# A two-layer hybrid attention block: score products in three float32r passes in place of plain float32

## The chip, the core and the metric

The kernel runs on one core of one Trainium2 chip. The core has five engines with queues of their own: TensorE (PE in the profile; its weight loads are listed apart as PEld), VectorE (DVE), ScalarE (ACT), GpSimd (POOL) and SyncE (SP), which here issues the transfers. Each engine takes its instructions in a fixed order and waits on semaphores for the others. Matrix products read SBUF, the 128-partition working memory, and write PSUM, eight banks of 512 float32 columns. The metric is the device time of one launch in microseconds, the median of several runs; lower is better.

## The reference, cut to what matters

Two layers over 512 tokens of width 1024, in float32. Each layer has an attention block with 16 heads of 64 (four with a top-k selection, four "stick-breaking", eight with a sliding window) and a gated feed-forward block. The score products are those between queries and keys, in four places:

```python
def _dsa(q, k, v, qi, ki, wi):                       # heads A, and the index heads
    ...
        rel = jax.nn.relu(jnp.einsum('bqhd,bsd->bqhs', qin, ki).astype(jnp.float32))
        score = jnp.einsum('bqh,bqhs->bqs', win.astype(jnp.float32), rel) * idx_scale
        ...
        _, sel = lax.top_k(score, n_sel)
        ...
        s = jnp.einsum('bqhd,bqkd->bhqk', qn, ks).astype(jnp.float32) * scale
...
def _stick_breaking(q, k, v):                        # heads B
    ...
        z = jnp.einsum('bqhd,bshd->bhqs', qn, k).astype(jnp.float32) * scale
...
def _swa_sinks(q, k, v, sinks):                      # heads C
    ...
        s = jnp.einsum('bqkgd,bskd->bkgqs', qn, kn).astype(jnp.float32) * scale
...
def reference(...):
    for l in range(DEPTH):
        ...
        x = x + g1 * _mixing(h, w_in[l], ..., w_o[l], cos, sin)
        h = _rms(x, ln2[l]) * (1 + sc2) + sh2
        x = x + g2 * _swiglu(h, w_gate[l], w_up[l], w_down[l])
    return x
```

## The kernel before, in words

Activations lie transposed, model dimension on the partitions and the 512 tokens along the free dimension. Every weight product is split: `load_w` (L535) fetches a chunk of weights into a `raw` slot, ScalarE copies it to float32r (the high part, L553) and VectorE subtracts (the low part, L554). `mm3` (L579) then does a product in three float32r passes: high by high, high by low, low by high. The activations are split the same way into `acth` and `actl`.

The score products are not split. After their projection, queries and keys are normalised and rotated on VectorE (`rope_apply`, L649), transposed by TensorE into a bank `w` (L255), and copied by ScalarE into float32 slots (L747, L748 for the index heads, L1016 and L1038 for heads C, L1142 and L1143 for heads A; `qk_run`, L871, scales those of heads B straight out of the product). A score product is then one float32 matmul with 64 rows (the head's dimension) and 128 to 512 columns of keys, or for heads B of queries, in `score` (L767), `headB` (L908), `unitC` (L1073) and `unitA` (L1167). Its bank `z` goes to ScalarE or VectorE: a relu and the weighted sum for the top-k search (L792, L793, sixteen rounds of eight on VectorE), the exponentials of heads B, the masked row maximum of heads C and A. The probabilities are transposed again (banks `t`) and multiplied by the values (bank `o`).

What sets the order: the class `Weaver` (L61) keeps a clock of its own, `now`, that each TensorE instruction moves by a price (L249), and a list of tasks. A task says how many nanoseconds its next step needs from now (the tables `LAT`, L52) and which banks; once its time has come, it goes ahead of the weight products, which fill the time between in packets of one `mm3`. So TensorE's order is fixed when the program is built. VectorE's own background work (the top-k rounds) is put in while its estimated backlog is under `SLACK`. SyncE issues transfers in order and waits for a free slot of the kind asked for; `wk` and `hid` share one pool of `WK` slots of 512 columns (L42, L208), used for modulation weights at the start (`mod_load`, L343), for queries, keys and selections in the attention, and for the hidden activations in the feed-forward block.

In the timeline, names give the tile: `z<-wk,wk` writes a score bank from two slots of that pool.

## Time and profile before

| | |
|---|---|
| median of 3 runs | 1319.72 us (1319.38 to 1322.63) |
| profiled execution: span from its first to its last instruction | 1314.4 us |
| TensorE busy | 1290.3 us, 98% |
| its weight loads | 1042.9 us, 79% |
| VectorE busy | 814.2 us, 62% |
| ScalarE busy | 540.0 us, 41% |
| chain that ended last | TensorE 95%, VectorE 2%, ScalarE 1% |
| read from memory | 149.34 MB |

The profile is one execution. For that execution the trace gives its span and no other time; the runs' median lies 5.3 us above the span, and that is the launch's time around the first and the last instruction. Matmuls are pipelined, so the busy time of TensorE counts overlaps and its own rate is read from the distance between starts. The stretches up to about 300 us and from 680 to 940 us are the two attention blocks; the rest is feed-forward.

### The profile page before, as it was taken

How to read it: one execution, taken by the hardware profiler on the slowest of the kernel's cores; microseconds unless marked ns; L12 is line 12 of the kernel's file. 1: busy time of each engine (PE TensorE's matmuls, PEld its weight loads, DVE VectorE, ACT ScalarE, POOL GpSimd, SP SyncE). 2: the span in 40 equal slices, each digit the busy share in tenths (PEclk: the TensorE clock that was granted, in tenths of full speed). 3: DMA queues.
4: the chain of work that ended last, by engine and by line, in shares of the span. 5: the costliest groups of instructions: out<-in, count | busy, mean ns of one | idle time of the engine just before them, and what ended most of it. 6: DMA issues, size and time to landing. Idle time of an engine off the chain costs nothing.

```text
span 1314.4 us, 19908 instructions
## 1 busy us (share of the span) xinstructions
PE 1290.3 (98%) x7572; PEld 1042.9 (79%) x7572; DVE 814.2 (62%) x2017; ACT 540.0 (41%) x1178; POOL 38.0 (3%) x51
## 2 busy tenths in 40 slices
PE   5999999999999999999999999999999999999998
PEld 3776787689888888888887868876998888888887
DVE  4898687857557667554259998786665533433423
ACT  4435576746322222222245466765452222222220
POOL 0000000002000000000020010000200000000000
PEclk9999999999999999999999999999999999999999
DMA  9852022220466667443222211121135422322311
GB/s 352 293 182 75 17 97 97 91 79 33 145 199 226 199 204 248 156 152 93 77 81 84 78 33 33 33 82 56 39 124 155 146 91 80 124 68 97 112 49 64
DMA packets 60000, 152.74 MB, mean 116 GB/s; under 512 B 7296, under 2 KB 7808, under 8 KB 59904
## 3 DMA queue, kind: packets, MB, share of 16 engines
q1 hardware_dynamic: 59904, 151.47, 35.2%
q8 instruction: 59, 0.97, 0.3%
q14 instruction: 37, 0.30, 0.1%
HBM read 149.34 MB, written 2.10 MB: 115 GB/s over the span
## 4 chain that ended last, share of the span: by engine, by line
PE 95%; DVE 2%; ACT 1%; issue 1%; DMA 0%; POOL 0%; POOLq 0%; SPq 0%; DVEq 0%; ACTq 0%
PE z L252 44%; PE mm L252 40%; PE o L252 4%; PE t L255 3%; PE w L255 2%; PE t L252 2%; PE w L252 1%; DVE sp L262 1%; DVE actl L262 1%; DVE e L262 0%; ACT ws L562 0%; DVE xT L262 0%; DMA xT<-in_x_dram 0%; ACT on L451 0%; ACT ws L553 0%
## 5 line engine op out<-in xcount | busy, mean ns | idle before, releaser
L252 PE MATMUL z<-acth,ws 128*128 128x512 f32 x1280 | 397.7, 390 | 0.0
L554 DVE TENSOR_TENSOR ws<-raw,ws 128x1024 fp32r<-128x1024 f32 (+3 forms) x190 | 208.0, 1098 | 249.1 <-ACT ws L553 249.0
L553 ACT CAST ws<-raw 128x1024 fp32r<-128x1024 f32 (+3 forms) x190 | 179.2, 948 | 334.7 <-PE z L252 157.2
L252 PEld LDWEIGHTS z<-acth,ws 128*128 128x128 f32 x1280 | 240.3, 188 | 49.8
L252 PE MATMUL mm<-hid,ws 128*128 128x512 f32 (+1 forms) x1212 | 271.8, 381 | 0.0
L252 PEld LDWEIGHTS mm<-hid,ws 128*128 128x128 f32 x1212 | 217.4, 188 | 48.5 <-issue 5.0
L252 PE MATMUL z<-actl,ws 128*128 128x512 f32 x640 | 249.0, 389 | 0.0
L252 PE MATMUL mm<-ws,acth 128*128 128x256 f32 (+2 forms) x704 | 151.8, 309 | 1.1 <-ACT acth L521 1.1
L252 PEld LDWEIGHTS z<-actl,ws 128*128 128x128 f32 x640 | 120.2, 188 | 24.5
L252 PE MATMUL mm<-acth,ws 128*128 128x256 f32 (+1 forms) x576 | 137.7, 325 | 0.5 <-DVE xT L262 0.5
L262 DVE SCALAR_TENSOR_TENSOR xT<-mm,mod,xT 128x512 f32<-128x512 f32 (+1 forms) x124 | 80.2, 660 | 68.5 <-PE mm L252 68.0
L252 PEld LDWEIGHTS mm<-ws,acth 128*128 128x128 f32 x704 | 111.0, 190 | 11.7 <-issue 5.6
L252 PEld LDWEIGHTS mm<-acth,ws 128*128 128x128 f32 x576 | 96.6, 190 | 14.3 <-issue 5.4
L252 PE MATMUL mm<-ws,actl 128*128 128x256 f32 (+2 forms) x352 | 104.0, 296 | 0.9 <-DVE actl L262 0.9
L252 PE MATMUL mm<-actl,ws 128*128 128x256 f32 (+1 forms) x288 | 91.8, 319 | 0.0
L291 ACT ACTIVATE e<-z 128x512 f32<-128x512 f32 x40 | 23.9, 599 | 159.6 <-PE z L252 159.6
L400 DVE SCALAR_TENSOR_TENSOR at<-nat,cs,at 128x512 f32<-128x512 f32 x98 | 73.1, 746 | 15.1 <-DMA nat<-in_w_mod_dram 14.8
L252 PEld LDWEIGHTS mm<-ws,actl 128*128 128x128 f32 x352 | 66.7, 190 | 1.6 <-DVE actl L262 1.5
L252 PE MATMUL z<-wk,wk 64*128 64x256 f32 (+3 forms) x192 | 57.4, 413 | 0.0
L252 PEld LDWEIGHTS mm<-actl,ws 128*128 128x128 f32 x288 | 54.9, 191 | 2.9
L793 DVE MATCH_REPLACE8 wk<-top,wk 128x256 f32<-128x256 f32 (+2 forms) x96 | 51.7, 543 | 0.0
L792 DVE MAX8 top<-wk 128x8 f32<-128x256 f32 (+2 forms) x96 | 50.8, 551 | 0.3
(213 smaller groups left out, 1411.0 us busy)
## 6 DMA issues: line engine op xcount, KB each, us to landing
raw<-in_w_gu_dram SPq DMA_DIRECT2D x88, 512.0 KB, 4.1
nat<-in_w_mod_dram SPq DMA_DIRECT2D x112, 256.0 KB, 3.4
raw<-in_w_dn_dram SPq DMA_DIRECT2D x48, 384.0 KB, 3.2
wk<-in_w_mod_dram SPq DMA_DIRECT2D x64, 256.0 KB, 5.5
raw<-in_w_nat_dram SPq DMA_DIRECT2D x16, 512.0 KB, 4.5
raw<-in_w_o_dram SPq DMA_DIRECT2D x16, 512.0 KB, 3.6
raw<-in_w_qk_dram SPq DMA_DIRECT2D x8, 512.0 KB, 4.4
raw<-in_w_mod_dram SPq DMA_DIRECT2D x8, 512.0 KB, 5.3
```

The costliest lines, as they stand in the source:

```text
L252: return self._done(T0.matmul(o, lhsT, rhs, **k), ns)
L255: return self._done(T0.transpose(o, i, idn), 109)
L262: ins = f(o, *a, **k)
L291: ins = S.activation(*a, **k)
L400: ins = V0.scalar_tensor_tensor(a, w, cs[:, k:k + 1], a, op0=OP.mult, op1=OP.add)
L553: ops = [S.copy(sp[:, 0, :n], raw[:, :n])]
L554: ops.append(V0.tensor_sub(sp[:, 1, :n], raw[:, :n], sp[:, 0, :n].bitcast(F32)))
L792: pinned(V0.max(top8, sc[:, :n]), n)
L793: pinned(V0.match_replace(sc[:, :n], top8, sc[:, :n], TAKEN), n)
```

## The change

Queries and keys are held in two float32r slots each, a high and a low part, and every score product is an `mm3`. A new helper does the split: ScalarE copies (or scales) out of PSUM into the high part, VectorE subtracts it from the source into the low part. The slots come from the `hid` kind, so more of the shared pool are in use, and `WK` grows from 17 to 25; the space comes out of a scratch area of the DMA set to 256 bytes. The values of heads B move from half of a `ws` slot to two `wk` slots. Comments are dropped. The prices in the `Weaver` and its `LAT` stay as they are, but the order follows from them anew, since a product now counts three instructions.

```diff
-NWS, NRAW, WK = 6, 5, 17
+NWS, NRAW, WK = 6, 5, 25
...
+    def split_to(hl, src, scale=None):
+
+        h, lo = hl
+        if scale is None:
+            S.copy(h, src)
+            V.tensor_sub(lo, src, h.bitcast(F32))
+        else:
+            S.mul(h, src, scale)
+            V.scalar_tensor_tensor(lo, src, scale, h.bitcast(F32), op0=OP.mult, op1=OP.subtract)
...
-                S.copy(a["kiT"][:, t * P:(t + 1) * P], tb[:, 2 * P:3 * P])
-                S.copy(a["qiT"][t].rearrange("p a b -> p (a b)"), tb[:, :2 * P])
+                split_to([k[:, t * P:(t + 1) * P] for k in a["kiT"]], tb[:, 2 * P:3 * P])
+                split_to([q[:, t * 256:(t + 1) * 256] for q in a["qiT"]], tb[:, :2 * P])
...
-                T.matmul(sb[:, :n], a["qiT"][t][hp, h // 2], a["kiT"][hp, :n], start=True, stop=True)
+                q0 = t * 256 + h // 2 * P
+                mm3(sb[:, :n], *(q[hp, q0:q0 + P] for q in a["qiT"]), *(k[hp, :n] for k in a["kiT"]), True, True)
...
-                a[name] = [slot("wk") for _ in range(2)]
-                yield from tr_run(ws, a["hs"], range(KO), lambda m, pb: S.mul(a[name][m], pb, scale), "qk")
+                a[name] = [[slot("hid") for _ in range(2)] for _ in range(2)]
+                yield from tr_run(ws, a["hs"], range(KO), lambda m, pb: split_to(a[name][m], pb, scale), "qk")
...
+        def vb_pre():
+            v = [slot("wk") for _ in range(2)]
+            a["vb"] = [v[t // 2][:, t % 2 * 256:(t % 2 + 1) * 256] for t in range(NT)]
...
-                        T.matmul(zb[:, a0:a0 + w], kT[:, j * P:(j + 1) * P], qT[:, j * P:], start=(a0 == 0), stop=False,
-                                 skip_group_check=True)
+                        mm3(zb[:, a0:a0 + w], *(v[:, j * P:(j + 1) * P] for v in kT), *(v[:, j * P:] for v in qT), a0 == 0,
+                            False, skip_group_check=True)
...
-                    S.copy(a["kcT"][g][:, t * P:(t + 1) * P], tb[:, g * P:(g + 1) * P])
+                    split_to([k[:, t * P:(t + 1) * P] for k in a["kcT"][g]], tb[:, g * P:(g + 1) * P])
...
-                    S.copy(a["qcT"][t][:, 2 * hf:2 * hf + 2].rearrange("p a b -> p (a b)"), tb[:, :256])
+                    split_to([q[:, 256 * hf:256 * hf + 256] for q in a["qcT"][t]], tb[:, :256])
...
-                    T.matmul(sb[:, hh * 256:hh * 256 + n], a["qcT"][t][hp, hs_[hh] // 2], a["kcT"][g][hp, k0:k0 + n],
-                             start=True, stop=True)
+                    q0 = hs_[hh] // 2 * P
+                    mm3(sb[:, hh * 256:hh * 256 + n], *(q[hp, q0:q0 + P] for q in a["qcT"][t]),
+                        *(k[hp, k0:k0 + n] for k in a["kcT"][g]), True, True)
...
-                S.copy(a["kaT"][:, t * P:(t + 1) * P], tb[:, 2 * P:3 * P])
-                S.copy(a["qaT"][t].rearrange("p a b -> p (a b)"), tb[:, :2 * P])
+                split_to([k[:, t * P:(t + 1) * P] for k in a["kaT"]], tb[:, 2 * P:3 * P])
+                split_to([q[:, t * 256:(t + 1) * 256] for q in a["qaT"]], tb[:, :2 * P])
...
-                T.matmul(sb[:, :n], a["qaT"][t][hp, h // 2], a["kaT"][hp, :n], start=True, stop=True)
+                q0 = t * 256 + h // 2 * P
+                mm3(sb[:, :n], *(q[hp, q0:q0 + P] for q in a["qaT"]), *(k[hp, :n] for k in a["kaT"]), True, True)
...
-    nc = _bacc.Bacc("TRN2", target_bir_lowering=False, num_devices=1)
+    nc = _bacc.Bacc("TRN2", target_bir_lowering=False, num_devices=1, dynamic_dma_scratch_size=256)
```

Three places in the order. The first is TensorE's at a unit of heads C in layer 0 (second half of the heads, third token block): the transposes of a query block into a bank `w`, and the next unit's two products into a bank `z`. Before:

```order
L255 MATMUL w_2399<-cst,nat_2274 128x128 x2
L252 MATMUL o_2403<-vc_1104,pT_2382 64x64 x4
L255 MATMUL t_2408<-cst,p_2295 128x128 x2
L252 MATMUL z_2443<-wk_1109,wk_1582 128x256 x2
L252 MATMUL o_2403<-vc_1104,pT_2411 64x64 x4
```

And of the changed kernel, the same place, which is also where a product comes soonest behind the split that it reads (`hid_1654` is the low part that VectorE makes from `w_2547`):

```order
L255 MATMUL w_2547<-cst,nat_2404 128x128 x2
L255 MATMUL t_2552<-cst,p_2430 128x128 x2
L252 MATMUL z_2587<-hid_1159,hid_1653 128x256
L252 MATMUL z_2587<-hid_1160,hid_1653 128x256
L252 MATMUL z_2587<-hid_1159,hid_1654 128x256
L252 MATMUL z_2587<-hid_1159,hid_1653 128x256
L252 MATMUL z_2587<-hid_1160,hid_1653 128x256
L252 MATMUL z_2587<-hid_1159,hid_1654 128x256
```

Two products of 64 rows have become six passes, and between the transposes into `w` and the first pass stand two other transposes alone, where four short products with the values stood as well.

The second is VectorE's at that place in the changed kernel; `p_2530` are the two masked row maxima (ISA) of the unit before, `nat_2561` the next query block.

```order
L262 ISA p_2530,cmx_2464<-z_2529,cst,rc_1648 128x256
L262 ISA cmx_2464 128x1
L262 ISA p_2530,cmx_2464<-z_2529,cst,rc_1648 128x256
L262 ISA cmx_2464 128x1
L262 TENSOR_TENSOR ocv_2496<-ocv_2496,ocd_2498 128x4
L262 TENSOR_REDUCE cvv_2559<-rt_2557 128x4
L262 TENSOR_TENSOR nat_2561<-mm_2420,gn 128x256
L262 SCALAR_TENSOR_TENSOR cnb_2465<-cmx_2464,nsk 128x2
L262 TENSOR_TENSOR hid_1654<-w_2547,hid_1653 128x256
```

The subtraction into `hid_1654` is new here and stands behind the row maxima and two instructions of the next query block.

The third is SyncE's at the start, from the second chunk of the first weight product on (`wk` are modulation weights, 256 KB each; `raw` weight chunks; `rp` the rope table; `gn` gains; `nsk` sinks). Before:

```order
L543 DMA raw_150<-in_w_nat_dram 128x972
L349 DMA wk_152<-in_w_mod_dram 128x512
L543 DMA raw_169<-in_w_nat_dram 128x648
L837 DMA rp<-in_rope_dram 128x512
L718 DMA gn<-in_gains_dram 128x512
L719 DMA nsk<-in_sinks_dram 128x16
L349 DMA wk_154<-in_w_mod_dram 128x512
L349 DMA wk_156<-in_w_mod_dram 128x512
```

Of the changed kernel:

```order
L543 DMA raw_150<-in_w_nat_dram 128x972
L349 DMA wk_152<-in_w_mod_dram 128x512
L349 DMA wk_154<-in_w_mod_dram 128x512
L349 DMA wk_156<-in_w_mod_dram 128x512
L349 DMA wk_158<-in_w_mod_dram 128x512
L349 DMA wk_160<-in_w_mod_dram 128x512
L349 DMA wk_162<-in_w_mod_dram 128x512
L349 DMA wk_164<-in_w_mod_dram 128x512
L349 DMA wk_166<-in_w_mod_dram 128x512
L543 DMA raw_169<-in_w_nat_dram 128x648
L349 DMA wk_171<-in_w_mod_dram 128x512
```

and further on, behind the fourth and the fifth group:

```order
L543 DMA raw_549<-in_w_nat_dram 128x1024
L543 DMA raw_554<-in_w_nat_dram 128x1024
L847 DMA rp<-in_rope_dram 128x512
L728 DMA gn<-in_gains_dram 128x512
L729 DMA nsk<-in_sinks_dram 128x16
```

The third group of modulation weights (from `wk_152` on) is no longer broken off behind its first transfer, the rope table and what follows it moved behind the fourth and fifth group and four chunks more.

## Rows read from the trace of the kernel before

**Rows 1.** The page: its span, and the chain that ended last, by engine.
```profile
span 1314.4 us, 19908 instructions
...
PE 95%; DVE 2%; ACT 1%; issue 1%; DMA 0%; POOL 0%; POOLq 0%; SPq 0%; DVEq 0%; ACTq 0%
```

**Rows 2.** Windows: stretch, its length, busy us per engine (instructions), clock, DMA share, GB/s.
```profile
40.00:140.00 100.00, 97.43 (x621) 69.35 (x620) 91.72 (x258) 49.32 (x108) 4.67 (x7) 0.98 0.43 152
680.00:800.00 120.00, 117.45 (x785) 91.25 (x785) 111.19 (x312) 66.03 (x154) 5.58 (x9) 1.00 0.17 54
```

**Rows 3.** Tile z: count, ns min/median/max, first and last start us, forms.
```profile
L252 PE MATMUL z<-wk,wk x192: 272/376/693, 96.6 to 857.4; 64*128 64x256 f32 x112, 64*128 64x128 f32 x48, 64*128 64x384 f32 x16, 64*128 64x512 f32 x16
L252 PE MATMUL z<-wk,ws x112: 272/482/693, 53.7 to 909.1; 64*128 64x256 f32 x32, 64*128 64x384 f32 x32, 64*128 64x512 f32 x32, 64*128 64x128 f32 x16
```

**Rows 4.** Timeline of PE: start us, us, line, out<-in, rows*columns, moving operand, count.
```profile
302.03 0.58 PE L252 MATMUL z<-ones,on 128*128 128x1 f32 x4
302.48 0.36 PE L252 MATMUL mm<-acth,ws 128*128 128x256 f32 x1
...
302.79 0.40 PE L252 MATMUL mm<-acth,ws 128*128 128x256 f32 x2
...
303.15 0.40 PE L252 MATMUL mm<-acth,ws 128*128 128x256 f32 x2
...
346.96 0.62 PE L252 MATMUL z<-acth,ws 128*128 128x512 f32 x2
...
347.64 0.62 PE L252 MATMUL z<-acth,ws 128*128 128x512 f32 x2
```

**Rows 5.** Timeline of PE: score products and what follows each.
```profile
181.62 1.13 PE L252 MATMUL z<-wk,wk 64*128 64x256 f32 x4
182.68 0.51 PE L252 MATMUL o<-vc,pT 128*64 128x64 f32 x10
...
188.90 0.71 PE L252 MATMUL z<-wk,wk 64*128 64x128 f32 x4
189.54 0.68 PE L252 MATMUL o<-vc,pT 128*64 128x64 f32 x15
...
257.44 1.12 PE L252 MATMUL z<-wk,ws 64*128 64x512 f32 x2
258.50 0.73 PE L252 MATMUL mm<-hid,ws 128*128 128x512 f32 x2
```

**Rows 6.** Groups of DVE by form: count, busy us, mean ns, idle before them.
```profile
L262 DVE TENSOR_TENSOR actl<-w,acth 128x512 fp32r<-128x512 f32 x8 | 5.5, 686 | 2.1 <-ACT acth L985 2.0
...
L262 DVE TENSOR_TENSOR actl<-w,acth 128x256 fp32r<-128x256 f32 x8 | 3.3, 418 | 0.9 <-ACT acth L985 0.9
```

**Rows 7.** Timeline, all engines: transposes of an output, the copy, the subtraction.
```profile
907.79 0.44 PE L255 MATMUL w<-cst,on 128*128 128x128 f32 x2
...
908.26 0.37 ACT L985 CAST acth<-w 128x256 fp32r<-128x256 f32 x1 [0.63 <-PE w L255]
...
908.67 0.42 DVE L262 TENSOR_TENSOR actl<-w,acth 128x256 fp32r<-128x256 f32 x1 [0.64 <-ACT acth L985]
```

**Rows 8.** Timeline of SP: issue of transfers.
```profile
18.94 0.33 SPq L349 DMA_DIRECT2D wk<-in_w_mod_dram  x1
...
22.39 9.77 SPq L349 DMA_DIRECT2D wk<-in_w_mod_dram  x15
```

**Rows 9.** Windows: the stretch in which the first weights arrive.
```profile
20.00:40.00 20.00, 19.97 (x115) 11.60 (x116) 14.06 (x37) 8.41 (x17) 0.00 (x0) 1.00 1.05 395
```

**Rows 10.** Chain of waits in order of time: start us, us, what.
```profile
45.21 0.94 DVE rt L262 x3
...
47.68 1.13 DVE ws L554
...
48.98 0.33 PE w L255
```

**Rows 11.** The page, DMA issues: count, KB each, us to landing.
```profile
wk<-in_w_mod_dram SPq DMA_DIRECT2D x64, 256.0 KB, 5.5
```

More of the change, by code (lines that the diff above doesn't have):

```diff
@@ L830, in idx_run @@
         def idx_run(ws):
-            a["kiT"] = slot("wk")
-            q = slot("ws").bitcast(F32)
-            a["qiT"] = a["qaT"] = [q[:, 0, t * 256:(t + 1) * 256].rearrange("p (a b) -> p a b", a=2) for t in range(NT)]
-            a["vb"] = [q[:, 1, t * 256:(t + 1) * 256] for t in range(NT)]
+            a["kiT"] = [slot("hid") for _ in range(2)]
+            q = slot("ws")
+            a["qiT"] = a["qaT"] = [q[:, i] for i in range(2)]
             a["wi"] = slot("wi")
@@ L886, in attention @@
         seg(lambda: load_w(w_qk[l, 0], KO, 256, None, st["late"] is not None, st["late"]), qk_run("qbT", 0.125))
-        seg(win_load(4), win_run(4, cons_vb, "v"))
+        seg(win_load(4), win_run(4, cons_vb, "v", vb_pre))
         seg(lambda: load_w(w_qk[l, 1], KO, 256), qk_run("kbT", 1.0))
@@ L893, in headB @@
             hp = slice((h % 2) * 64, (h % 2) * 64 + 64)
-            qT, kT = a["qbT"][h // 2][hp], a["kbT"][h // 2][hp]
+            qT, kT = ([v[hp] for v in a[name][h // 2]] for name in ("qbT", "kbT"))
             acc = None
@@ L997, in c_pre @@
             a["vc"] = [slot("vc") for _ in range(NT)]
-            a["kcT"] = [slot("wk") for _ in range(2)]
+            a["kcT"] = [[slot("hid") for _ in range(2)] for _ in range(2)]
         def cons_kc(t, pb):
@@ L1048, in qc_pre @@
             a["rc"] = slot("rc")
-            a["qcT"] = [slot("wk", (P, 4, P)) for _ in range(NT)]
+            a["qcT"] = [[slot("hid") for _ in range(2)] for _ in range(NT)]
             a["onC"] = [None] * NT
@@ L1122, in a_pre @@
             a["va"] = [slot("va") for _ in range(NT)]
-            a["kaT"] = slot("wk")
+            a["kaT"] = [slot("hid") for _ in range(2)]
             a["ra"] = slot("ra")
```

## The prediction

> **What bounds the kernel now.** I read the page first: its span, and the chain of waits by engine. The span is 1314.4 us and TensorE makes up 95% of the chain that ended last [rows 1]; all other engines together have 5%. So the time is the length of TensorE's own stream, and a change is worth what it takes out of that stream or what holes it tears into it. The windows by stage come next: VectorE has the least room of the others, busy 91.72 of 100 us in the first attention stage and 111.19 of 120 us in the same stage of the second layer [rows 2]. These two stages are where more VectorE work could be felt. Last, the tile view of the score bank and the timeline of TensorE give the prices of a product before and after.
>
> **The score products.** The trace records a float32 product as two instructions. The tile view has 192 and 112 of them with 64 rows [rows 3], so halved: 32 products of 128 columns, 72 of 256, 24 of 384 and 24 of 512, the two layers together. Each becomes three float32r passes.
>
> What a product costs now: a unit of the sliding-window heads holds two products, so four instructions. From its first start to the start of what follows are 1.06 us at 256 columns and 0.64 us at 128 [rows 5]. The difference, 0.42 over four instructions, is 0.105 for each 128 columns. A product with a single column of moving data takes 0.45 / 4 = 0.112 us apiece [rows 4]: no weight load and product get below that, so I price the 128-column instruction at 0.112. Then 0.64 - 4 x 0.112 = 0.19 us belongs to going from full-height weights to 64-row weights and back, once for each run of such products. The 512-column product confirms it: (1.06 - 0.19) / 2 = 0.435 for one instruction [rows 5]. So a float32 product is 0.224, 0.43, 0.65 and 0.86 us at 128, 256, 384 and 512 columns.
>
> What a pass will cost: the weight products of this kernel are float32r already. Three in a row start 0.36 us apart at 256 columns, 0.120 each, and 0.68 us apart at 512 columns, 0.227 each [rows 4]; 384 lies midway at 0.174. No row shows float32r at 128 columns. From below it is the 0.112 of the weight load; from above the rate of four passes, as if the type gained nothing there, 128 columns in 0.213 us (the 256-column price of a two-pass instruction). I take 0.112, the row that it is nearest to. Three passes are then 0.336, 0.36, 0.52 and 0.68 us.
>
> The difference: 32 x (+0.112) + 72 x (-0.07) + 24 x (-0.125) + 24 x (-0.179) = 3.6 - 5.0 - 3.0 - 4.3 = -8.7 us. The switches at 0.19 stay: 107 runs of 64-row products in the order before, 108 now. With the 128-column pass at 0.213 it is 32 x 0.416 = 13.3 in place of 3.6, and the sum is +1.0.
>
> Rows 5 show the 512-column float32 product at about twice 0.43, which is four times 512 columns at 2.4 GHz. The Trainium skill (FP8 and Floating Point Precision, TensorE Precision Notes) says that true float32 makes four passes through the array, and the trace agrees: by the passes alone, three in place of four, one pass less for all 44,032 columns would be worth 18.3 us (an estimate from that page). That is a rival below.
>
> **VectorE's splits.** Each of 36 copies per layer out of the transposes (or out of the query and key products) gets a subtraction behind it on VectorE; ScalarE's copy stays and only writes another type. At most 0.418 us for those up to 256 columns, 0.686 for 512 [rows 6]: 64 x 0.418 + 8 x 0.686 = 32 us of VectorE work. None of it is on TensorE's path by its length, since TensorE has weight products to do; it costs where a score product stands soon behind its split. The same pair stands in the trace already, where the outputs are transposed: transposes begin at 907.79, the copy runs 908.26 to 908.63, the subtraction from 908.67 to 909.09 [rows 7]. So a split is ready 1.3 us behind the start of its transposes, where the copy alone was ready after 0.84, and later if VectorE is busy.
>
> The order of TensorE now has 34 places where a product is the first to read a fresh split. Counted in the prices of rows 4 and 5, the work between runs from 0.4 us to 8 us: one place with 0.4 (second excerpt of the change), thirteen with 1.3 to 1.7, the others more. At the first one VectorE has two row maxima over 256 columns, a reduction and a 256-column product standing ahead of the split: 4 x 0.418 = 1.7 us, of which I count 1.5 as a hole. At the thirteen a hole opens once VectorE is more than some 0.3 us late; I take 0.3 us each, 3.9 in all. Together +5 us, from 0 (VectorE prompt everywhere) to 13 + 1.5 = 14.5 (a microsecond late at each). What is queued behind a late product is all of TensorE's stream, since it takes its work in order. What waits in front of the split on VectorE waits for ScalarE's copy; behind it stand the row maxima that the softmax needs, so a VectorE that runs ahead idles here.
>
> **The start.** The pool of 512-column slots grows from 17 to 25. The third group of modulation weights now finds its slots at once: before, its first transfer goes at 18.94 and the other seven wait for slots until 22.39 [rows 8]. In the new order they stand ahead of a weight chunk (332 KB), the rope table and the gains (262 KB each). With the DMA moving 395 GB/s there [rows 9], 0.86 MB less ahead is 2.2 us. TensorE's product with this group is the first that waits for it, so up to 2.2 us can come off its stream here. Against that, the rope table moves behind 8.7 MB: 9.0 MB with itself from 18.94 on, 22.8 us at that rate, plus some 4 to 5.5 us to landing [rows 11]: 46 to 47. VectorE began the rope at 45.21 and the transposes ended their wait at 48.98 [rows 10]. Two weight splits of 1.13 us [rows 10] that lay between the two now stand ahead of the rope, so some 1.5 of those 3.8 us are left from the rope to the transposes: 47.5 to 48.5 against 48.98. I take -1.0, from -2.2 to +2 should the table come later still.
>
> The scratch size, the values' new place and the dropped comments cost nothing: the same copies and the same SyncE transfers stand in the order.
>
> **The sum.** -8.7 + 5 - 1 = -4.7 us in the profiled execution: a span of 1309.7. The runs' median of 1319.72 lies 5.3 us above that span; what lies around the span stays, and so 1315.
>
> **The rivals.**
> One: the 128-column pass at 0.213. For it speaks that no float32r product here is under 256 columns wide, so nothing bears out my price; against it that the floor of 0.112 is seen on a float32 product. +9.7: 1325.
> Two, slower: VectorE becomes the bound between 40 and 140 us and between 680 and 800 us. It has 8.3 and 8.8 us left there [rows 2]. About twenty splits per layer fall in: 16 x 0.418 + 4 x 0.686 = 9.4 us, and each may hold the engine idle for the copy (0.64 us in rows 7; half of it on average gives 6.4). It decides from the point where 15.8 outgrows 8.3: 7 us per layer, 14 in all, 1329. Against it: much of VectorE's work there is the top-k search, which is needed only later.
> Three: neither the floor nor the 0.013 us by which a float32r product exceeds its columns applies to 64-row weights, and every product gets a quarter cheaper. Without the floor they cost 32 x 0.21 + 72 x 0.43 + 24 x 0.65 + 24 x 0.86 = 74 us; a quarter is 18.5 in place of 8.7: 1305. Against it: both are seen at 128 rows in rows 4.
> Four: weight loads of the passes are not hidden. The four instructions of a unit in rows 5, each with a load of its own into the same 64 rows, fit into 1.06 us without a load's 0.112 between them, so it should not be. If it came with the new type, 152 more instructions at 0.112 are 17 us: 1332. The Trainium skill (TensorE: Matmul & The Clock Gate, Part 3: Packing small matmuls) has loads overlap products in flight only when their row groups differ; the trace does not bear this out for float32, and shows no 64-row float32r.
> Five: nothing changes, 1320, if TensorE's gain is filled by holes elsewhere.
>
> **How the numbers follow.** Forecast 44%, one 24%, two 16%, three 10%, four 4%, five 2%. A measurement of this kernel tells 0.3% from no change, 4 us: faster is under 1315.7, slower over 1323.7. The forecast's own range is 1309 to 1321, and its middle lies at the edge: 55% faster, 43% same. One is half same, half slower; two mostly slower; three faster; four slower. That gives 0.37, 0.33 and 0.30. The range reaches from rival three to rival two: 1305 to 1329.
>
> **What would show it.** Right: in the new profile a 64-row float32r product of 256 columns starts 0.120 us behind the one before, of 512 columns 0.227, of 128 columns 0.112; TensorE's idle time behind VectorE's splits sums to about 5 us, the longest at one product of the third token block in layer 0; the transposes of the first token block begin before 48.98; the feed-forward stages last as long as before. Wrong: a 128-column pass of 0.2 us or more, idle time of TensorE behind splits of 15 us or more, VectorE without gaps in the two stages named, or a gain that sits in the feed-forward stages.

## The result, and the profile after

The changed kernel takes 1355.07 us, median of 4 runs (1350.63 to 1356.54), beside 1321.18 of the kernel before (1319.38 to 1323.64): a ratio of 1.0265, interval 1.0234 to 1.0296. The forecast was 1315 and the range ended at 1329, so the change costs 34 us where a gain of 5 was expected.

The page of the changed kernel's profiled execution, the lines that answer to rows 1, and the granted clock in 40 slices:

```profile
span 1354.7 us, 20268 instructions
...
PEclk9898999999999999999998999988999999999999
...
PE 86%; DVE 8%; ACT 2%; DMA 2%; issue 1%; POOL 0%; SPq 0%; POOLq 0%; DVEq 0%; ACTq 0%
```

The span is 40.3 us longer than in rows 1. VectorE now has 8% of the chain that ended last, where it had 2% [rows 1]. And TensorE's clock, which was at its lower level (1.2 GHz) for 3.4 us of the span before, is there for 55.6 us: the eights in the clock's row. The loss sits in the two attention stages. Cut at the same instructions of both traces (ScalarE's table loads near the stages' borders, at 318.43, 648.14 and 953.56 us before and 333.92, 664.11 and 993.84 after, and the start of the last product), the time up to the first feed-forward stage is 333.9 us in place of 318.4, and that of the second layer's attention 329.7 in place of 305.4. The feed-forward stages are as long as before (330.2 and 357.1 us against 329.7 and 357.0).

What TensorE waits for in the changed kernel (engine, line, what it waited for; us in all, times, longest):

```profile
...
PE z L252 <- ACT ws L588: 6.4, 7, 2.4
PE w L255 <- DVE nat L262: 3.9, 2, 3.1
PE z L252 <- DVE sp L262: 3.5, 3, 1.9
PE w L255 <- DVE ws L262: 3.0, 1, 3.0
PE w L255 <- DVE actl L262: 2.4, 1, 2.4
PE z L252 <- DVE ws L262: 2.3, 4, 1.4
PE z L252 <- DVE hid L262: 1.6, 2, 1.0
...
```

The lines with ws and hid are the split queries and keys: 6.4 + 3.0 + 2.3 + 1.6 = 13.3 us that did not exist before (13.9 with 0.6 us on ScalarE's `hid`, further down). One such wait from the timeline of all engines (start us, us, engine, line, out<-in, count, and in brackets the idle time before it with what ended it):

```profile
717.22 0.49 PE L255 MATMUL w<-cst,nat 128*128 128x128 f32 x3
717.25 0.50 DVE L262 TENSOR_TENSOR nat<-rt,rt 128x320 f32<-128x320 f32 x1
...
717.65 2.37 DVE L554 TENSOR_TENSOR ws<-raw,ws 128x1024 fp32r<-128x1024 f32 x2
...
718.36 0.25 ACT L588 CAST hid<-w 128x128 fp32r<-128x128 f32 x1
...
720.02 0.96 DVE L262 TENSOR_TENSOR rt<-o,rp 128x320 f32<-128x320 f32 x3
720.06 0.39 PE L252 MATMUL mm<-acth,ws 128*128 128x512 f32 x1
720.88 1.23 DVE L554 TENSOR_TENSOR ws<-raw,ws 128x1024 fp32r<-128x1024 f32 x1
721.01 0.17 ACT L751 ACTIVATE wi<-o 128x4 f32<-128x4 f32 x1 [2.40 <-DVE rt L262]
722.01 0.30 DVE L262 TENSOR_TENSOR hid<-w,hid 128x128 fp32r<-128x128 f32 x1
...
722.35 0.37 ACT L588 CAST ws<-w 128x256 fp32r<-128x256 f32 x1 [1.16 <-DVE hid L262]
...
722.86 0.42 DVE L262 TENSOR_TENSOR ws<-w,ws 128x256 fp32r<-128x256 f32 x1
...
723.42 0.52 PE L255 MATMUL w<-cst,nat 128*128 128x128 f32 x3 [2.97 <-DVE ws L262]
```

Two things delay the split here. The key's high part is ready at 718.6, but VectorE, in order, does two weight splits, the rope of another block and a third weight split first and comes to the key's low part at 722.01. And ScalarE's copy of the query's high part, which needs no result of VectorE, waits for that subtraction (1.16 us). Ahead of it ScalarE had already stood 2.40 us at an instruction for another block, which waits for VectorE's rope. ScalarE and VectorE read the same bank of transposes, and the program keeps them apart: copy, subtraction, copy, subtraction, each waiting for the one before. The single bank for transposes is free only at 723.3, 5.6 us behind the last transpose; TensorE stands at the next block's transposes for 2.97 us. The Trainium skill (PSUM — Partial Sum Buffer, "PSUM bank collisions raise a hardware error") says that the compiler's back end adds a dependency between any two instructions on different engines that touch the same bank and the same 32 partitions of it, two reads as well; the trace agrees, with ScalarE's 1.16 us above, a read that waits for a read.

This is one of the longest delays, but the others are late as well. From the end of the last transpose to the end of the last split the median is 2.6 us in 16 groups of three blocks (two splits from one bank; 5.6 and 6.6 us are the longest) and 2.0 us in 24 groups of two. Of those 24, the eight with two splits have 3.1 us and the sixteen with one split 1.4. Before, the copies of a three-block group were done 0.58 us behind the transposes wherever no engine was late. The planner still sends TensorE to the products 1.05 us behind the transposes.

Rows 2 have VectorE as the engine nearest to its limit. Windows of the same stages now, with the columns of rows 2 (busy us of PE, PEld, DVE, ACT, POOL, then the granted clock):

```profile
60.00:100.00 40.00, 39.94 (x227) 29.24 (x226) 33.60 (x99) 14.37 (x28) 0.00 (x0) 0.91 0.48 170
100.00:140.00 40.00, 38.13 (x231) 28.12 (x229) 31.81 (x88) 19.11 (x41) 2.90 (x5) 0.87 0.24 80
...
720.00:760.00 40.00, 35.56 (x192) 27.96 (x192) 34.79 (x96) 15.29 (x32) 0.00 (x0) 0.91 0.28 84
760.00:800.00 40.00, 38.29 (x275) 29.78 (x273) 31.88 (x97) 20.75 (x47) 2.83 (x5) 1.00 0.13 37
800.00:840.00 40.00, 37.51 (x309) 31.09 (x308) 39.32 (x138) 24.39 (x70) 1.94 (x3) 1.00 0.18 54
```

VectorE has 5 to 8 us free in the first four, and is full only from 800 to 840. So it is late at single splits rather than short of time over the stages. The granted clock stands at 0.87 to 0.91 in three of the five; rows 2 have 0.98 and 1.00.

The products themselves, in the answers to rows 5 (timeline of TensorE):

```profile
182.90 0.97 PE L252 MATMUL z<-hid,hid 64*128 64x256 f32 x6
183.80 0.45 PE L252 MATMUL o<-vc,pT 128*64 128x64 f32 x8
...
200.12 0.89 PE L252 MATMUL z<-hid,hid 64*128 64x128 f32 x6
200.94 0.69 PE L252 MATMUL o<-vc,pT 128*64 128x64 f32 x16
...
81.27 0.96 PE L252 MATMUL z<-hid,ws 64*128 64x512 f32 x3
82.16 0.50 PE L252 MATMUL mm<-ws,acth 128*128 128x256 f32 x2
```

Two products of 256 columns take 0.90 us where rows 5 have 1.06, two of 128 columns 0.82 where they have 0.64, and one of 512 columns 0.89 with the change of weights, as the prediction's 0.68 + 0.19. By the prediction's prices the first two would be 0.91 and 0.86. The prices were right.

### The profile page after: what moved, and what is told of

It is laid out like the page before. It is cut to its first block, busy times and chain, and to the rows that moved or that the text cites. A ratio compares the mean times of both kernels' runs of the same rounds, so it can differ in the third digit from the quotient of the medians.

```text
span 1354.7 us, 20268 instructions
## 1 busy us (share of the span) xinstructions
PE 1308.0 (97%) x7724; PEld 1076.5 (79%) x7724; DVE 835.0 (62%) x2089; ACT 542.2 (40%) x1178; POOL 38.0 (3%) x51
## 4 chain that ended last, share of the span: by engine, by line
PE 86%; DVE 8%; ACT 2%; DMA 2%; issue 1%; POOL 0%; SPq 0%; POOLq 0%; DVEq 0%; ACTq 0%
PE z L252 41%; PE mm L252 36%; PE o L252 4%; PE t L255 2%; PE w L255 2%; PE t L252 1%; DVE sp L262 1%; PE w L252 1%; DVE rt L262 1%; DVE ws L554 1%; DVE nat L262 1%; DVE actl L262 1%; DVE top L803 1%; DMA wk<-in_w_mod_dram 1%; DVE wk L804 0%
## 5 line engine op out<-in xcount | busy, mean ns | idle before, releaser
L252 PE MATMUL mm<-hid,ws 128*128 128x512 f32 (+1 forms) x1212 | 274.8, 384 | 0.2 <-DVE xT L262 0.2
L252 PE MATMUL mm<-ws,acth 128*128 128x256 f32 (+2 forms) x704 | 154.9, 314 | 1.6 <-ACT acth L521 1.1
L252 PE MATMUL mm<-acth,ws 128*128 128x256 f32 (+1 forms) x576 | 143.7, 334 | 0.5 <-DVE xT L262 0.5
L252 PEld LDWEIGHTS mm<-acth,ws 128*128 128x128 f32 x576 | 99.5, 195 | 13.6 <-issue 3.8
L252 PE MATMUL z<-hid,hid 64*128 64x256 f32 (+3 forms) x288 | 54.5, 318 | 2.3 <-DVE hid L262 1.6
```

The costliest lines, as they stand in the source:

```text
L252: return self._done(T0.matmul(o, lhsT, rhs, **k), ns)
```

## The experiments

Every run has a span and a mean granted clock. Where TensorE's stream is the time, a stretch at half clock costs half its length; so the span times the clock is about what the run would have taken at full clock, and (1 - clock) x span x 2 its time at half clock. The last two columns of the table are these, as medians over the runs of a kernel. They split a loss into waits and clock, roughly: the clock is on record to a thousandth, which is 0.7 us of the last column for a single run and 1.3 us of the one before. Each ratio is to the runs of the kernel before made in the same group; the changed kernel's is to the 1321.18 above, and to the 1317.75 of the table its loss is 37 us rather than 34.

| kernel | median us (runs) | ratio to before, 95% interval | us at half clock | span at full clock |
|---|---|---|---|---|
| before (first group of runs) | 1317.75 (19) | 1 | 8 | 1313.1 |
| changed | 1355.07 (4) | 1.0265 [1.0234, 1.0296] | 51 | 1326.3 |
| start alone | 1320.16 (10) | 1.0006 [0.9982, 1.0031] | 11 | 1313.8 |
| passes alone | 1327.15 (10) | 1.0062 [1.0041, 1.0083] | 29 | 1311.3 |
| splits alone | 1359.55 (4) | 1.0316 [1.0257, 1.0374] | 43 | 1334.9 |
| pairs | 1342.22 (4) | 1.0157 [1.0102, 1.0211] | 39 | 1319.9 |
| late due | 1330.45 (4) | 1.0085 [1.0057, 1.0114] | 28 | 1314.0 |
| pairs due | 1337.67 (4) | 1.0146 [1.0123, 1.0170] | 37 | 1316.8 |
| holes | 1368.48 (4) | 1.0387 [1.0359, 1.0416] | 46 | 1343.2 |
| holes filled | 1352.90 (4) | 1.0267 [1.0241, 1.0294] | 11 | 1345.5 |
| pairs late | 1327.22 (6) | 1.0061 [1.0034, 1.0088] | 24 | 1313.9 |
| late more | 1339.92 (4) | 1.0150 [1.0103, 1.0197] | 41 | 1317.2 |
| tuned | 1331.48 (4) | 1.0111 [1.0063, 1.0159] | 25 | 1317.0 |
| tuned rope | 1327.45 (6) | 1.0071 [1.0048, 1.0095] | 20 | 1316.2 |
| passes order | 1317.18 (12) | 0.9992 [0.9974, 1.0011] | 14 | 1308.1 |
| after order | 1356.43 (4) | 1.0321 [1.0271, 1.0372] | 58 | 1325.5 |
| pairs order | 1339.03 (4) | 1.0157 [1.0122, 1.0192] | 35 | 1320.7 |
| heads b | 1324.08 (11) | 1.0047 [1.0029, 1.0065] | 16 | 1314.1 |

**One part of the change at a time.** The start alone, on the kernel before:

```diff
-NWS, NRAW, WK = 6, 5, 17
+NWS, NRAW, WK = 6, 5, 25
-    nc = _bacc.Bacc("TRN2", target_bir_lowering=False, num_devices=1)
+    nc = _bacc.Bacc("TRN2", target_bir_lowering=False, num_devices=1, dynamic_dma_scratch_size=256)
```

> The kernel before, with 25 working buffers in place of 17 and the smaller scratch: only the order of the first transfers moves (rope table behind the modulation weights, as in the changed kernel); products stay float32, no split of queries and keys. Theory H (holes: TensorE waits for late operands and then runs at the lower clock for a while): one hole of about 3 us near 47 us, 10 us of half clock after it as in the changed kernel (49.8-53.2, 60.1-66.9), so 1319.7 + 2 + 5 = about 1326 us (1322 to 1330). Rival S (the start is the whole loss): 1345 or more. Rival P (the three passes cost more than priced, or pull the clock down by themselves): 1320, no half clock near 50 us.

It is no different from the kernel before, and 0.7 us longer at full clock. H's 1322 to 1330 is missed: the wait of 3.08 us at the first transposes is there, with 3.4 us at half clock around its end, but the time hardly shows it, and the kernel before has such a stretch too, at 100 us. The start is not the loss.

Passes alone, on the changed kernel (the score products call mms):

```diff
         if scale is None:
             S.copy(h, src)
-            V.tensor_sub(lo, src, h.bitcast(F32))
...
+    def mms(out_ap, lh, ll, rh, rl, first, last_, **kw):
+        mm3(out_ap, lh, lh, rh, rh, first, last_, **kw)
```

> The changed kernel without the subtractions: three passes per product, all of them on the high parts (the low parts are left out of the computation); the same order on TensorE and the same start. H: passes give 8.7 us back, the start costs about 6, the other holes go: about 1317 us (1311 to 1326), half clock only near 50 and 60 us and at the end. P: 1345 or more, half clock as in the changed kernel. S: 1345 or more with the loss before 100 us.

A miss: 10 us above the expectation, with 29 us at half clock, though at full clock the passes do gain (1313.8 to 1311.3). That was taken up again below.

Splits alone:

```diff
+    def mms(out_ap, lh, ll, rh, rl, first, last_, **kw):
+        T.matmul(out_ap, ll.bitcast(F32), rh.bitcast(F32), start=first, stop=last_, **kw)
```

> The changed kernel with all its splits, but one float32 product in place of the three passes, low part of one operand by high part of the other (the other two terms are left out of the computation); TensorE still waits for VectorE's subtraction. H: the loss stays, and the passes' gain of 8.7 us is lost too: 1350 to 1365 us, 30 us or more at half clock. P: about 1326 us (the start alone), little half clock.

As the theory of holes has it: 1359.55, with products at their old price. With one product in place of three passes the planner returns to the order of the kernel before: TensorE's instructions follow each other as in the run with the start alone, and the two kernels differ by the splits (and by the new place of heads B's values). So this pair gives the price of the splits directly: 1320.16 to 1359.55, 39 us, of which 21.1 are there at full clock (1313.8 to 1334.9) and about (43 - 11) / 2 = 16 are clock. What the three passes save beside the splits has to be read from a kernel in the same order, further down.

Both high parts first, on the changed kernel (the same for the shared keys and the first attention):

```diff
-                split_to([k[:, t * P:(t + 1) * P] for k in a["kiT"]], tb[:, 2 * P:3 * P])
-                split_to([q[:, t * 256:(t + 1) * 256] for q in a["qiT"]], tb[:, :2 * P])
+                split_two([k[:, t * P:(t + 1) * P] for k in a["kiT"]], tb[:, 2 * P:3 * P],
+                          [q[:, t * 256:(t + 1) * 256] for q in a["qiT"]], tb[:, :2 * P])
...
+    def split_two(hl1, src1, hl2, src2):
+        S.copy(hl1[0], src1)
+        S.copy(hl2[0], src2)
+        V.tensor_sub(hl1[1], src1, hl1[0].bitcast(F32))
+        V.tensor_sub(hl2[1], src2, hl2[0].bitcast(F32))
```

> The changed kernel, but where two splits read one bank of transposes (first attention, selection scores, shared keys) ScalarE makes both high parts first and VectorE then both low parts; in the changed kernel the second high part waits on VectorE's first subtraction. All else is as changed. H with the chain of four steps as the main cause of late splits: a third to a half of the loss comes back, 1335 to 1345 us, and the last split of a three-block group ends 1.3 to 1.6 us after its last transpose in place of 2.1 to 5.6. H with VectorE's queue as the main cause: 1350 to 1355. P: 1355.

13 us come back, and the last split of a three-block group ends 1.5 us (median) behind its last transpose. TensorE's order is that of the changed kernel, instruction by instruction, so nothing but the order of copies and subtractions has moved. The chain of four steps is about a third of the loss.

**The planner, and the clock.** Due times raised, on the changed kernel, in the tables of both layers:

```diff
-    ev=1045
+    ev=2700
...
-    oT=2208
+    oT=3200
```

> The changed kernel with two of the planner's due times raised: products after a split 2700 ns behind the transposes in place of 1045, the transposes' bank given back after 3200 ns in place of 2208; nothing else is edited. In the changed kernel the last split of a three-block group ended 2.6 us (median of 16) behind its last transpose, of a two-block group 2.0 us (median of 24). Theory H (TensorE is sent to its products too early): most holes go, TensorE takes weight products in the time: span times granted clock 1326 to 1316 us, half clock 51 to 25 us, 1328 to 1338 us. Rival V (VectorE's work itself is too much in these stages): the wait only moves, 1350 or more.

24.6 us come back, about two thirds of the loss, by two numbers in the planner's table; no engine does less work. TensorE's waits on splits in this kernel, all of them:

```profile
PE w L255 <- DVE ws L262: 2.8, 2, 2.3
...
PE z L252 <- DVE hid L262: 0.2, 1, 0.2
```

13.3 us have become 3.0. So this part of the loss is not VectorE's amount of work, but that TensorE's order did not allow for when it is done. One reservation: new due times make a new order of TensorE as a whole, and a new order alone moved the kernel with passes alone by 10 us (further down).

> Both high parts first (as in the run before) and the planner's due times raised to what was measured there: products 1900 ns behind the transposes, the bank given back after 2500 ns. H: holes as in the kernel before, so what is left of the gain of the three passes shows: 1318 to 1328 us. Rival P (short passes pull the clock down by themselves, as the run with passes alone had 29 us at half clock against 11): 1325 to 1332 with 25 us or more at half clock.

The edit is ev=1900 and oT=2500 on top of both high parts first. At 1337.67 it is a miss for both theories, whose ranges end at 1328 and 1332. It is 4.5 us under the run with both high parts first, within the spread of the two (1332.31 to 1344.66 and 1335.97 to 1338.65), and behind the longer due times. That 1900 ns covers the median split and not the late ones is the likely reason; it was not tested.

Eight empty waits in the feed-forward stages of the kernel before:

```diff
+    def hole(pb, pb2, w, act):
+        t_ = slot("e")
+        S.copy(t_, pb)
+        for _ in range(4):
+            S.copy(t_, t_)
+        T._done(T0.matmul(pb2[:, :1], t_[:, :P], t_[:, :1], start=True, stop=True), 0)
```

> The kernel before with eight waits added in the feed-forward stages, where it had none: ahead of the second half of four gate-and-up products in each layer TensorE waits for five copies of 512 columns on ScalarE one after the other (about 3 us). Nothing of the change is in it. H (a hole pulls the clock down behind it): 8 x 3 = 24 us and in addition 10 to 20 us of clock, 1354 to 1364 us, 25 us or more at half clock in these stages. Rival P: 24 us and no more, 1344 us, no half clock there.

And the same with the wait filled:

```diff
         for _ in range(4):
             S.copy(t_, t_)
+        for _ in range(14):
+            T._done(T0.matmul(pb2, w, act, start=True, stop=True), 0)
```

> The same eight waits, but ahead of each TensorE makes 14 products of 512 columns that nobody reads (3.2 us), so that it works while the copies go on. H: the holes' own time stays, the clock's part goes: 1340 to 1348 us, half clock as in the kernel before. Rival P: the same time as with empty holes.

The windows around the first of the eight, with empty waits and then with filled ones (columns as in rows 2):

```profile
424.00:430.00 6.00, 5.91 (x27) 4.55 (x25) 4.25 (x7) 1.62 (x3) 0.00 (x0) 1.00 0.77 258
430.00:434.00 4.00, 0.46 (x3) 0.46 (x3) 0.00 (x0) 3.39 (x6) 0.00 (x0) 0.96 0.28 88
434.00:438.00 4.00, 4.00 (x15) 3.19 (x15) 0.00 (x0) 0.00 (x0) 0.00 (x0) 0.62 0.01 4
```

```profile
424.00:430.00 6.00, 6.00 (x29) 4.95 (x28) 5.13 (x7) 2.00 (x3) 0.00 (x0) 1.00 0.55 181
430.00:434.00 4.00, 4.00 (x19) 3.34 (x18) 0.24 (x1) 2.40 (x5) 0.00 (x0) 1.00 0.71 224
434.00:438.00 4.00, 3.54 (x19) 2.67 (x19) 0.00 (x0) 1.05 (x2) 0.00 (x0) 1.00 0.00 0
```

With the wait empty TensorE has 0.46 us of work in four, and then, though it has products to do without a break, its clock stands at 0.62 on average over the next four: half clock for most of them. All eight waits (3.65 us each, 29.2 in all) have such a stretch of 3.4 or 6.8 us at their end or behind it. Filled, none has. The empty waits cost 50 us, 29 as waits and most of the rest (19 by the table) by the clock; with throwaway products in their place it is 35. Both are 4 to 5 us above the ranges expected, since a wait is 3.65 us long and not 3; the difference of 15.6 us between them is what decides, and the rival had it at nothing. That a hole in TensorE's stream can cost its length and a stretch at half clock as well is shown by this pair, on a kernel that has nothing of the change. That the shorter holes of the changed kernel do the same is inferred from where its stretches lie.

**A version that is faster than both?** None came of these four. The edits of pairs and of late due together:

> Both high parts first, and the planner's due times of the run that gave most back (2700 and 3200 ns). The two edits remove the same waits (the run with due times alone came to 1330, both high parts first with 1900 and 2500 ns to 1338). Theory H (waits for late splits are the loss): 1322 to 1330 us, no wait of TensorE on a split over 1 us but for the one at the start of the second layer. Rival V (VectorE as a whole is too late, whatever the order of the copies): 1330 to 1338.

Late due with two more due times:

```diff
-    z=4066
+    z=5000
...
-    A=1632
+    A=2500
```

> The changed kernel with due times 2700 and 3200 ns as before, and two more raised that VectorE's added work delays as well: the softplus chain (4066 to 5000 ns, second layer 3536 to 4600) and the first attention's probabilities (1632 to 2500, second layer 1517 to 2300). H: the waits near 115, 239 and 765 us (2.0, 2.3 and 1.1 us in the run with 2700 and 3200 alone) go, 1322 to 1328 us. V: 1330 or more, the waits move.

All of it, with due times of 2400 and 2700 ns, and splits ahead in VectorE's order:

```diff
     def split_two(hl1, src1, hl2, src2):
+        with lab(LAB[0], -950000):
```

> All of it: both high parts first, splits ahead of the weights' splits in VectorE's order, due times 2400 and 2700 ns, the softplus chain and the probabilities later as in the run before. H: what the passes save shows: 1312 to 1322 us. V: 1328 or more.

Then the rope table's transfer, moved from its old place:

```diff
         st["wm"] = [mod_load(0, 0, True)]
+        with lab("?", -900000):
+            nc.sync.dma_start(rp, rope)
```

> As the run before, and the rope table's transfer right behind the first set of modulation weights, so that the 3 us wait near 46 us goes. H: 2 to 5 us less than without (no wait, and no half clock at 50 us). Rival (the start's slack, as the order of the first transfers alone made no difference): within 1.5 us of it.

Both high parts first with the long due times is the best of the whole kernels with splits, 1327.22, beside 1327.45 of the last. At full clock they stand 1 and 3 us above the kernel before. "Late more" is a plain miss: longer due times for two more chains made it 9 us slower than without, with 13 us more at half clock. The rope table in front shortens the wait at 46 us from 3.1 to 0.9 us and gave 4 us over the run without it, by medians of runs whose ranges overlap (1326.40 to 1330.98, and 1329.50 to 1339.24). "All of it" came to 1331.48, where rival V had 1328 or more and H 1312 to 1322. So these runs do not exclude that VectorE's added work itself keeps a part of the loss, once the late splits are out of the way.

**TensorE's order held.** The run with passes alone had left open whether the passes pull the clock down. Here the planner prices a pass at a third of the float32 product, so that TensorE's order is that of the kernel before, a product's three passes standing where its one product stood:

```diff
+            if lhsT.shape[0] == 64 and rhs.dtype == F32R:
+                ns = max(n / 0.6, 209) / 3
```

> Passes alone as before (all three on the high parts, the low parts left out of the computation), but the planner prices a pass at a third of the float32 product, so that TensorE's order is that of the kernel before, each product replaced by its three passes in place. Theory O (the planner's new order made the waits): 1320 less 8.7 = 1311 us (1309 to 1315), half clock as in the kernel before. Theory P (the passes pull the clock down by themselves): 1320 to 1327 us with 20 us or more at half clock.

> The changed kernel whole, with the same price for a pass: TensorE's order is that of the kernel before, the splits and their waits are all there. If the planner's new order was a part of the loss beside the late splits: 1342 to 1350 us. If the late splits are all of it: 1352 to 1360 us.

> As the run before, with both high parts made first. Without that price it came to 1342 us. O: 1328 to 1337 us. Late splits alone: 1340 us or more.

Passes alone in the old order: 1317.18, the same as the kernel before within the interval, with 14 us at half clock; at full clock 5.7 us less than the start alone. It lies between the two theories' numbers, and the clock speaks for the order: 10 us of the earlier miss were the planner's new order. But with the splits in, the order makes no difference: 1356.43 beside 1355.07. Nor does it with both high parts first: 1339.03 beside 1342.22, with the same ratio of 1.0157; that number too lies between O's range and the 1340 of late splits alone. Passes alone and the whole change, both in the old order, differ from each other by the subtractions and the low parts alone, and 39 us lie between them, as between the start alone and the splits alone. The three passes beside the splits can now be read as well, from the splits alone to this kernel: 1334.9 to 1325.5 at full clock, 9.4 us. By the medians it is 3.1 us (1359.55 to 1356.43), with more time at half clock (58 us in place of 43). TensorE's waits on VectorE's nat, passes alone in the old order (none of its waits names ws or hid):

```profile
PE w L257 <- DVE nat L264: 4.2, 2, 3.2
...
PE mm L254 <- DVE nat L264: 0.3, 1, 0.3
```

and on nat, ws and hid with the splits in:

```profile
PE w L257 <- DVE nat L264: 5.6, 3, 3.1
PE z L254 <- ACT ws L590: 4.9, 5, 2.2
PE w L257 <- DVE ws L264: 4.8, 2, 3.0
...
PE z L254 <- DVE hid L264: 2.0, 4, 0.7
...
PE z L254 <- DVE ws L264: 1.3, 2, 0.9
```

13 us of waits on splits and on their bank (4.9 + 4.8 + 2.0 + 1.3) appear with the subtractions. By the table, 17.4 of the 39 us are there at full clock (1308.1 to 1325.5) and (58 - 14) / 2 = 22 are clock.

Last, the second attention's products alone, on the start alone (and the price of a pass as above):

```diff
-                yield from tr_run(ws, a["hs"], range(KO), lambda m, pb: S.mul(a[name][m], pb, scale), "qk")
+                yield from tr_run(ws, a["hs"], range(KO), lambda m, pb: split_to(a[name][m], pb, scale), "qk")
...
-                        T.matmul(zb[:, a0:a0 + w], kT[:, j * P:(j + 1) * P], qT[:, j * P:], start=(a0 == 0), stop=False,
-                                 skip_group_check=True)
+                        mm3(zb[:, a0:a0 + w], *(v[:, j * P:(j + 1) * P] for v in kT), *(v[:, j * P:] for v in qT), a0 == 0,
+                            False, skip_group_check=True)
```

> Only the second attention's products (32 of 152, 8 each of 128 to 512 columns) in three passes, their splits with the projections of 512 columns, where the planner leaves several us before the first product; the rest of the scores stays float32, TensorE's order and the start as in the run with the start alone. H (the loss is where a split lies close before its product): no new wait; the passes save 2.1 us here: 1316 to 1320 us, the same as the kernel before within what can be measured.

1324.08, above the expected 1316 to 1320. None of its waits names a split, as expected; but one on a copy of the keys and values is new (1.0 us), and at full clock it equals the start alone (1314.1 and 1313.8). With 32 of 152 products there was little to gain. Its profiled execution has 10.2 us at half clock, at 101.9 and 753.9 us, with TensorE at work on these products and no wait above 0.11 us in the 8 us ahead; the start alone has none there. That is worth about 5 us, the size of the miss.

## Why the prediction was wrong, step by step

- **The score products, -8.7.** Right. Rival one (a 128-column pass at 0.213) and rival four (loads not hidden) fall with the rows above: six passes of 128 columns and two changes of weights fit into 0.82 us. Rival three falls too, since 256 columns do not get a quarter cheaper. Measured at full clock, in the old order each time: 9.4 us beside the splits (splits alone to after order), 5.7 without them (start alone to passes order), where some of it turns into other waits.
- **VectorE's splits, +5 (0 to 14.5).** This is the step that failed: the wait behind the splits, counted at 5 and at 14.5 at most, with nothing for the clock. In the same order of TensorE the subtractions cost 39 us, 17.4 of them at full clock (21.1 by the pair with float32 products). At the one place that the sum names it was about right: of 1.5 us, 0.59 came as a wait, and the six passes behind it took 1.54 us in place of 0.97.

```profile
212.81 1.54 PE L252 MATMUL z<-hid,hid 64*128 64x256 f32 x6 [0.59 <-ACT hid L588]
```

  The rest came elsewhere, and three things in the working were off. It took a split as one copy and one subtraction, as in rows 7; but 24 groups split twice out of one bank, and there the second copy waits for the first subtraction. Rows 7 could not show this, since an output is split once. It counted VectorE's queue at one place and 0.3 us at thirteen; the last splits end 2.0 to 2.6 us behind the transposes in the median, 5.6 and 6.6 at the worst. In the case shown, weight splits and rope stand ahead of them. And it looked at the products behind a split, not at the next transposes, which wait for the bank (3.0 us at 723.4).
- **What the sum left out: the clock.** Every hole was counted at its length. Of the changed kernel's loss at the median, 13.2 us are left at full clock (1313.1 to 1326.3), and (51 - 8) / 2 = 21.5 are the lower clock. Even with the holes sized rightly the sum would have come to 1333 or so. Rows 2 gave little cause to look, with 0.98 and 1.00; the 0.98 is one stretch of 3.4 us at 100 us.
- **The start, -1.0 (-2.2 to +2).** Inside its bounds: +0.7 at full clock. The rope table came later than forecast; VectorE began on it at 48.66 (45.21 in rows 10):

```profile
48.66 0.95 DVE L262 TENSOR_TENSOR rt<-mm,rp 128x320 f32<-128x320 f32 x3 [1.55 <-DMA rp<-in_rope_dram]
...
50.29 0.87 PE L255 MATMUL w<-cst,nat 128*128 128x128 f32 x3 [3.09 <-DVE nat L262]
```

  The transposes begin at 50.29, not before 48.98 as the sign for it had asked. So the number held although a wait of 3.1 us came that the working had excluded; that is luck in part. It hardly costs, as TensorE was there sooner too.
- **Rival two** had the right direction and engine, and a figure of 1329, but not the mechanism: VectorE is not the bound in the two stages, it keeps gaps. With due times that fit its lateness most of the loss goes, with the same work on it. What the 1331.48 of "all of it" leaves open is said above.
- **The signs.** Idle time behind splits of 15 us or more was the sign for wrong, and it came close: 13.9 us on the new splits, where 5 would have been right. (2.4 us more stand behind an output's split, but passes alone has these too, without any new split.) The starts of the passes came as forecast, VectorE kept gaps, and the feed-forward stages stayed as long as before.

What stays open: 9 us between the best version with splits and the kernel before. 8 of them are clock by the table ((24 - 8) / 2), and at full clock the 8.7 us of the passes go, by count and not by a test, on waits that remain (5.6 us at two transposes that wait for their operand, 2.3 on the probabilities of the first attention, 1.7 on a split's bank; the kernel before has 1.6 us of such waits). Whether a full fit of the planner's table would bring the gain out was not tried.

## What to carry to other kernels

In a stream that one engine works through in order, a change that makes an operand later by a microsecond needs the planner's due time for that operand changed with it; two numbers in a table were worth 25 us here, about two thirds of the loss. To price one part of a change, compare kernels in which TensorE's order is the same: a new order alone was worth 10 us. Before costing a second reader of a PSUM bank, ask who else reads the bank: a copy and a subtraction from one bank do not overlap, and two such pairs form a chain across two engines. And a hole in TensorE's stream may cost more than its length (50 us for 29 us of waits in the run with empty holes).

## What was not expected of the hardware

- The lower clock came beside short waits: the changed kernel has nine stretches of 3.4 to 10.2 us before its end, and the nearest wait at or ahead of their beginning is from 0.5 to 3.1 us long. But not every wait brings it. The run "late more" stands as long as the others at 46 us and has no half clock near it.
- It also came without a long wait ahead. In the run with passes alone no gap of TensorE between 200 and 245 us is over 0.6 us, yet the clock is at half from 245.4 to 262.4 (columns as in rows 2):

```profile
240.00:245.00 5.00, 4.13 (x29) 2.84 (x27) 5.00 (x18) 4.62 (x14) 0.00 (x0) 1.00 0.76 232
245.00:250.00 5.00, 4.48 (x20) 3.15 (x19) 4.11 (x21) 2.01 (x8) 0.00 (x0) 0.54 0.70 233
250.00:262.00 12.00, 12.00 (x48) 8.39 (x47) 4.85 (x14) 4.12 (x12) 0.00 (x0) 0.50 0.01 4
```

  TensorE is busy throughout the last 12 us and stays at 1.2 GHz. The kernel before passes the same place at full clock, with a wait of 0.7 us there. No run here tells why.
- At the second attention's products it came with no wait at all, in the kernel before too, while TensorE ran 64-row score products between weight products (the kernel before, then both high parts first; columns as in rows 2):

```profile
92.00:100.00 8.00, 8.00 (x37) 5.59 (x36) 7.53 (x19) 3.27 (x6) 0.00 (x0) 1.00 0.41 137
100.00:104.00 4.00, 4.00 (x19) 0.90 (x19) 3.67 (x9) 2.57 (x5) 0.00 (x0) 0.57 0.00 0
```

```profile
742.00:750.00 8.00, 8.00 (x42) 6.46 (x41) 7.79 (x21) 3.69 (x5) 0.00 (x0) 1.00 0.17 51
750.00:757.00 7.00, 7.00 (x33) 6.18 (x33) 5.24 (x13) 3.67 (x8) 0.00 (x0) 0.54 0.18 56
```

  In the second layer, nine of the thirteen kernels with three passes have such a stretch, beginning between 750.4 and 757.4 us with at most 0.25 us of waits in the 8 us ahead, and none of the five with float32 products does; in the first layer both kinds have them. So the passes may lower the clock there by themselves, which no run here isolates; the changed kernel has no such stretch, and all of its nine lie at waits.
- From run to run of one kernel the time at half clock varies: 8 to 24 us in the 12 runs of passes in the old order, 0 to 21 in 19 of the kernel before. Most of the spread of the times is this: the span at full clock stays within 2.7 us in the one and 3.5 in the other.
